# A decoder trunk's mixer: rotary rows exchanged by small transfers instead of a matrix, forget gates placed behind the keys

## The chip, the cores and the metric

One core of a Trainium2 chip. TensorE is called PE, its weight loads PEld, VectorE DVE, ScalarE ACT, GpSimd POOL and SyncE SP; every engine works through its own queue in order. The metric is the time of one execution on the device in microseconds (us), the median of several.

## The reference, cut to what matters

One decoder layer for 256 tokens of width 1024: a norm, a wide input projection, two token mixers side by side (forgetting attention, called fox, with 8 heads, and sparse attention, called nsa, with 8 query heads on 2 key groups), a gated merge, then an expert layer found by product keys, and a last norm. All in float32. The parts that the change touches:

```python
def apply_partial_rope(x, cos, sin):            # of 64 columns of a head the first 16
    xr = x[..., :ROPE_DIM].astype(jnp.float32)
    x1, x2 = xr[..., :half], xr[..., half:]     # 8 and 8
    rot = jnp.concatenate([x1 * c - x2 * s, x1 * s + x2 * c], axis=-1)
    ...
# hybrid_mixer
log_f = jax.nn.log_sigmoid(f_logit + fox_f_bias)         # forget gates, c = cumsum(log_f) in fox_attention
q_nsa = apply_partial_rope(heads(nq, NSA_HEADS), cos, sin)
k_slc = apply_partial_rope(heads(ksl, NSA_GROUPS), cos, sin)
k_win = apply_partial_rope(heads(kwn, NSA_GROUPS), cos, sin)
k_cmp, v_cmp, cmp_end = compress_kv(...)                 # 15 overlapping blocks of 32 tokens through a small MLP
gates = jax.nn.sigmoid(nsa_gate_logit)
```

## The kernel before, in words

Every weight matrix is streamed from memory in blocks of 512 KB. The list `order` (lines 155 to 161) gives their order: the transposed input projections `w_t` (compressed keys and values, selected and window keys, nsa queries, fox queries and keys), natural ones (`w_sv`, `w_fv`), the merge gates `w_m`, and then the branch, output and expert weights up to the end. One call of `slot` (line 228) handles one block: SP fetches blocks two and three ahead into three `raw` buffers, ACT makes the rounded high part `whi` of the block two ahead (L185) and DVE the rest `wlo` (L189), and PE multiplies the present block in three passes (high with high, high with low, low with high), 24 matmuls of 256 columns at L356 for a transposed block. `pair` takes two blocks for one PSUM bank and hands the evacuation of the bank to the list `early`, which runs at the start of the next slot.

All other work of the mixer is put by hand between the blocks: the tuples `pre` that `pair` and `natural` get are functions that run in that slot after the low part and before the slot's matmuls, in the order written. `tick` in a tuple moves the attention heads on by one: it runs first in its slot (before the low part), and issues the values of the head two back, the scores of two new heads on every other call, a softmax on DVE and ACT, and the transposition of the last probabilities. There are 24 heads: 16 nsa heads, which read the rotated queries `nqs`, and 8 fox heads, which add the forget sums `cleft` and `crt` to their scores.

The steps that the change touches, in the order of the slots (lines 783 to 803):

- `start_tables` (L431): the reciprocal norm of each token, spread over the partitions by PE, is copied three times from PSUM by DVE (L347, L433, L434), and the cosine and sine tables are multiplied by it (L435, L436).
- `rope_in` (L452): ACT evacuates a pair (selected and window keys "k", query halves "q0" and "q1"), the tile `ropein`. `rope` (L457): PE multiplies it by a signed exchange matrix `rt` (L460, PSUM out), DVE multiplies that by the sine table (L462) and the evacuated rows by the cosine table (L463), adds them (L465), and `halve` makes the high part on ACT (L449) and the low part on DVE (L450). `swap` (L468) then copies the keys' two halves of the partitions into each other by two transfers on POOL's queue.
- The compression: `cmp_windows` (DVE, L481) lays out the 15 overlapping windows of the keys and of the values, `cmp_hidden` (PE L488, ACT L492) is the first layer with weights that `w1_load` brings by four transfers of 512 KB on SP's queue, `back` (L496) transposes the hidden layer on PE; `cmp_keys`, `cmp_values`, `cmp_scores`, `cmp_turn` and `cmp_out` (L703, two matmuls at L706) follow.
- The forget gates: `fg_log`, `fg_rest` (the reciprocals of the gates and the remainder of the logarithm, L561 to L567), `fg_logs`, `fg_sums` (four matmuls at L578, copies on ACT, low parts on DVE at L584) and eight `fg_left` (L587), one masked copy of the sums for each fox head.

In the kernel before, the pair "q0" has `fg_rest`, the keys' rotary, `swap`, the second windows and the third load in its second slot; the pair "q1" has the two hidden layers, with the transposition of the first (`cmp_back`) ahead of the second, and q0's rotary; the first fox pair has `fg_sums` and q1's rotary.

Of the kernel before, what the change touches and what calls it, by code (L numbers as in the profile page):

```python
# [19 lines left out]
P = 128  # L20
# [17 lines left out]
def _constants():  # L38
# [3 lines left out]
    for b in (0, 64):  # L42
        for i in range(8):
            rt[b + 8 + i, b + i] = -1.0
            rt[b + i, b + 8 + i] = 1.0
    inv = np.power(f(500000.0), -np.arange(0, 16, 2, dtype=f) / f(16)).astype(f)

    def table(pos):
        ang = pos.astype(f)[:, None] * inv[None, :]
        c = np.ones((P, len(pos)), f)  # L50
        s = np.zeros((P, len(pos)), f)
        for b in (0, 64):
            for o in (0, 8):
                c[b + o:b + o + 8] = np.cos(ang).T
                s[b + o:b + o + 8] = np.sin(ang).T
        return c, s
# [75 lines left out]
def body(tc, nc, a):  # L132
# [12 lines left out]
    def bank(tag):  # L145
        return ps.tile([P, 512], F32, name=tag, tag=tag)

    def halves(t):
        return t.rearrange("p (j t) -> p j t", j=2)
# [192 lines left out]

    def spread(r, out):
        rb = bank("pO")
        for b in range(2):
            nc.tensor.transpose(rb[:, b * P:(b + 1) * P], r[:, b:b + 1].to_broadcast([P, P]), ident)
        nc.vector.tensor_copy(out, rb[:, :T])  # L347
        return rb
# [82 lines left out]
    def start_tables():  # L431
        rb = spread(rn[0], rs)
        nc.vector.tensor_copy(rsk[0:64], rb[0:64, :T])  # L433
        nc.vector.tensor_copy(rsk[64:128, 0:T - 1], rb[64:128, 1:T])  # L434
        nc.vector.tensor_tensor(ctab, ctab, rs, OP.mult)  # L435
        nc.vector.tensor_tensor(stab, stab, rs, OP.mult)  # L436
# [11 lines left out]
    def halve(hi, lo, src):  # L448
        nc.scalar.activation(hi, src, AF.Copy)  # L449
        nc.vector.tensor_tensor(lo, src, hi.bitcast(F32), OP.subtract)  # L450

    def rope_in(name, pj, scale):  # L452
        raw = wk.tile([P, 2, T], F32, name="ropein")
        nc.scalar.activation(raw, halves(pj), AF.Copy, scale=scale)
        ropes[name] = raw

    def rope(name, dst, parts):  # L457
        raw = ropes[name]
        rp = bank("pS")
        nc.tensor.matmul(rp, K["rt"], flat(raw), start=True, stop=True)  # L460
        t = wk.tile([P, 2, T], F32, name="ropetmp", bufs=1)
        nc.vector.tensor_tensor(t, halves(rp), stab[:, None, :].to_broadcast([P, 2, T]), OP.mult)  # L462
        nc.vector.tensor_tensor(raw, raw, ctab[:, None, :].to_broadcast([P, 2, T]), OP.mult)  # L463
        dst = raw if dst is None else dst
        nc.vector.tensor_tensor(dst, raw, t, OP.add)  # L465
        halve(*parts, dst)
# [18 lines left out]
    def cmp_hidden(j):  # L485
# [10 lines left out]
        def back():  # L496
            tp = bank("pO")
            nc.tensor.transpose(tp[:, :30], hn, ident[:30, :30])
            nc.vector.tensor_copy(ht[j], tp[:, :30])
        backs.append(back)  # L500

    backs = []

    def cmp_back():
        run(backs)

# [52 lines left out]

    def fg_rest():  # L560
        nc.vector.tensor_scalar(gate, gate, 1.0, None, OP.add)  # L561
        nc.vector.reciprocal(gate, gate)
        nc.vector.tensor_scalar(yr, y1, -1.0, None, OP.add)
        nc.vector.tensor_tensor(ea, ea, yr, OP.subtract)
        nc.vector.reciprocal(yr, y1)
        nc.vector.tensor_tensor(ea, ea, yr, OP.mult)
        nc.vector.tensor_scalar(z, z, 0.0, None, OP.min)  # L567
# [134 lines left out]

    def cmp_out():  # L703
        for b in range(2):
            o = bank("pT")
            nc.tensor.matmul(o, cptb[:, b], flat(vbd), start=True, stop=True)  # L706
            nc.scalar.activation(y[:, b, 1], o, AF.Copy)

# [69 lines left out]
    def sv_evac(acc):  # L778
# [10 lines left out]
    pair(lambda pj: rope_in("q0", pj, 0.125), ah, al,  # L789
         pre=((fg_log, lambda: cmp_windows(0)), (lambda: table(AF.Gelu), fg_rest, lambda: rope("k", None, (krope[:, 0, 0], krope[:, 1, 0])), swap, lambda: cmp_windows(1), lambda: w1_load(1, 0))))  # L790
    pair(lambda pj: rope_in("q1", pj, 0.125), ah, al,
         pre=((lambda: cmp_hidden(0), fg_logs, lambda: w1_load(1, 1)), (cmp_back, lambda: cmp_hidden(1), lambda: rope("q0", nqt[:, 0:2], (nqs[:, 0, 0:2], nqs[:, 1, 0:2])))))
    lefts = [lambda h=h: fg_left(h) for h in range(H)]
    pair(fox_evac(fqt, 0, 0.125), ah, al, ((), ()),
         ((cmp_keys, fg_sums, cmp_back, tick, cmp_copies), (tick, lambda: rope("q1", nqt[:, 2:4], (nqs[:, 0, 2:4], nqs[:, 1, 2:4])))))
    pair(fox_evac(fqt, 1, 0.125), ah, al, ((), ()), ((cmp_keys_rope, tick), (cmp_values, tick, lefts[0])))
    pair(fox_evac(fkt, 0, 1.0), ah, al, ((), ()), ((tick, cmp_scores), (tick, lefts[1], lefts[2])))
    pair(fox_evac(fkt, 1, 1.0), ah, al, ((), ()), ((tick, cmp_turn, lefts[3]), (tick, cmp_out, lefts[4], lefts[5])))
    natural(512, (0, 2, 4, 6, 8), value_evac(vf, 512), lambda k: (),
            lambda k: ((tick, lefts[6]), t2, t2, (tick, lefts[7]))[k])  # L800
    for m in range(8):
        pre = [[tick], [tick]]
        if m == 5:
            pre = [[tick, lambda: y_turn(1, 0)], [tick, lambda: y_turn(1, 1)]]
# [503 lines left out]
```

## Time and profile before

| | us |
|---|---|
| median of 3 runs | 1036.61 |
| lowest, highest | 1035.8, 1037.08 |
| the profiled execution, its own time | 1037.04 |
| span of its profile, first to last instruction | 1035.3 |
| PE busy in the span | 1024.0 |
| DVE, ACT, POOL busy in the span | 768.2, 526.3, 17.9 |

The granted clock of PE is 0.997 of full speed over the span. Busy times of engines lie side by side and do not add up to the span. A matmul's duration contains its passage through the array, so matmuls in a row overlap, and the distance of two starts tells more than a duration. The mixer's part with the pairs listed above lies between about 20 and 175 us; what follows are PE-bound projections and the expert layer.

### The profile page before, as it was taken

Reading aid. Unit: us, or ns where it says so; the run is one execution under the profiler, and the core shown is the slowest. Engines: PE = TensorE matmul, PEld = TensorE weight load, DVE = VectorE, ACT = ScalarE, POOL = GpSimd, SP = SyncE. Lnnn points to the kernel's source line nnn. Section 1 sums busy time; section 2 is a strip of 40 time slices with the busy share of each in tenths; the row PEclk is TensorE's granted clock in tenths of the full one; section 3 lists DMA queues with packets and bytes.
Section 4 is the critical chain, followed back from the end, with each engine's and each line's share of the span. In section 5 each row is a group of like instructions: output and inputs, shape, how many; then the busy total and the mean of one; then the engine's idle time right before and its main releaser. Section 6 shows DMA issues by size and latency. Waiting matters only on the chain.

```text
span 1035.3 us, 18645 instructions
## 1 busy us (share of the span) xinstructions
PE 1024.0 (99%) x7369; PEld 947.8 (92%) x7369; DVE 768.2 (74%) x1454; ACT 526.3 (51%) x841; POOL 17.9 (2%) x31
## 2 busy tenths in 40 slices
PE   9999999999999999999999999999999999999997
PEld 7898999999999999999999999988888888888885
DVE  5788677876798879779889999966666666666664
ACT  7554445565644464644444444445454545555554
POOL 3000010000000000000000000000000000000000
PEclk9999999999999999999999999999999999999998
DMA  8733444566455546554444445445555555555662
GB/s 268 242 101 104 123 121 128 174 189 202 150 189 192 182 152 204 168 199 163 161 149 159 150 159 164 163 163 190 196 192 195 192 195 194 192 197 189 199 208 102
DMA packets 51319, 180.09 MB, mean 174 GB/s; under 512 B 5808, under 2 KB 7232, under 8 KB 51232
## 3 DMA queue, kind: packets, MB, share of 16 engines
q1 hardware_dynamic: 48816, 175.27, 51.8%
q0 software_dynamic: 832, 1.99, 0.8%
q10 hardware_dynamic: 1584, 1.64, 0.5%
q8 instruction: 58, 0.95, 0.4%
q14 instruction: 29, 0.24, 0.1%
HBM read 176.79 MB, written 1.05 MB: 172 GB/s over the span
## 4 chain that ended last, share of the span: by engine, by line
PE 93%; DVE 3%; ACT 2%; DMA 1%; issue 1%; SPq 0%; DVEq 0%; ACTq 0%
PE pj L356 50%; PE acc L1208 34%; PE pw L1161 3%; PE pS L647 1%; PE pT L619 1%; PE pS L488 1%; PE pS L1069 1%; DMA raw<-in_w_t 1%; DVE wlo L189 1%; DMA xg<-in_x 1%; ACT whi L185 1%; PE pO L630 0%; PE pO L631 0%; PE pj L749 0%; PE pj L750 0%
## 5 line engine op out<-in xcount | busy, mean ns | idle before, releaser
L189 DVE TENSOR_TENSOR wlo<-raw,whi 128x1024 fp32r<-128x1024 f32 (+2 forms) x329 | 398.9, 1213 | 133.6 <-ACT whi L185 132.6
L185 ACT ACTIVATE whi<-raw 128x1024 fp32r<-128x1024 f32 (+2 forms) x329 | 342.9, 1044 | 164.7 <-PE pj L356 123.6
L356 PE MATMUL pj<-ah,whi 128*128 128x256 f32 x1344 | 336.1, 288 | 0.0
L356 PE MATMUL pj<-al,whi 128*128 128x256 f32 x1344 | 329.9, 283 | 0.1
L356 PEld LDWEIGHTS pj<-al,whi 128*128 128x128 f32 x1344 | 257.4, 192 | 1.8 <-issue 1.0
L356 PEld LDWEIGHTS pj<-ah,whi 128*128 128x128 f32 x1344 | 257.0, 191 | 1.5 <-issue 1.2
L356 PE MATMUL pj<-ah,wlo 128*128 128x256 f32 x1344 | 189.1, 283 | 0.0
L356 PEld LDWEIGHTS pj<-ah,wlo 128*128 128x128 f32 x1344 | 173.6, 192 | 0.0
L1208 PE MATMUL acc<-whi,ch 128*128 128x512 f32 x512 | 158.5, 389 | 0.0
L1208 PE MATMUL acc<-whi,cl 128*128 128x512 f32 x512 | 158.5, 389 | 0.0
L1208 PE MATMUL acc<-wlo,ch 128*128 128x512 f32 x512 | 158.2, 389 | 0.0
L1196 ACT ACTIVATE ch<-G 128x256 fp32r<-128x256 f32 x128 | 53.4, 418 | 171.2 <-PE acc L1208 171.2
L1208 PEld LDWEIGHTS acc<-whi,cl 128*128 128x128 f32 x512 | 96.1, 188 | 20.3 <-DVE cl L1197 0.3
L1208 PEld LDWEIGHTS acc<-whi,ch 128*128 128x128 f32 x512 | 96.0, 188 | 20.1 <-ACT ch L1196 0.3
L1208 PEld LDWEIGHTS acc<-wlo,ch 128*128 128x128 f32 x512 | 96.1, 188 | 19.9
L1197 DVE TENSOR_TENSOR cl<-G,ch 128x256 fp32r<-128x256 f32 x128 | 54.4, 425 | 69.5 <-ACT ch L1196 69.5
L1173 ACT ACTIVATE G<-pw 128x512 f32<-128x512 f32 (+31 forms) x32 | 12.5, 392 | 73.5 <-DVE G L1171 73.5
L356 PE MATMUL pj<-bh,whi 128*128 128x256 f32 x192 | 48.1, 286 | 0.0
L356 PE MATMUL pj<-bl,whi 128*128 128x256 f32 x192 | 47.5, 283 | 0.0
L1153 DVE TENSOR_TENSOR oha<-oha,wt 128x1024 f16<-128x1024 f16 x64 | 44.3, 692 | 2.2
L356 PEld LDWEIGHTS pj<-bl,whi 128*128 128x128 f32 x192 | 36.8, 192 | 0.0
L356 PEld LDWEIGHTS pj<-bh,whi 128*128 128x128 f32 x192 | 36.8, 192 | 0.0
(278 smaller groups left out, 824.7 us busy)
## 6 DMA issues: line engine op xcount, KB each, us to landing
raw<-in_u_t SPq DMA_DIRECT2D x128, 512.0 KB, 3.4
raw<-in_v_n SPq DMA_DIRECT2D x128, 512.0 KB, 3.2
raw<-in_w_m SPq DMA_DIRECT2D x16, 512.0 KB, 3.6
raw<-in_w_q SPq DMA_DIRECT2D x16, 512.0 KB, 3.8
raw<-in_w_t SPq DMA_DIRECT2D x15, 512.0 KB, 4.6
raw<-in_w_b SPq DMA_DIRECT2D x8, 512.0 KB, 3.6
raw<-in_w_o SPq DMA_DIRECT2D x8, 512.0 KB, 3.5
sg<-in_w SPq DMA_DIRECT2D x4, 512.0 KB, 6.7
```

The source lines that it names most:

```text
L185: return [lambda s=slice(u, min(v, n)): nc.scalar.activation(hi[:, s], raws[k][:, s], AF.Copy) for u, v in cuts]
L189: nc.vector.tensor_tensor(lo[:, cs], raws[k][:, cs], hi[:, cs].bitcast(F32), OP.subtract)
L356: nc.tensor.matmul(out, (wl if v == 2 else wh)[:, c], (l if v == 1 else h)[:, c], start=(i == 0), stop=(i == len(seq) - 1))
L488: nc.tensor.matmul(hp[:30, :P], flat(wins[j][:, lp // 8, lp % 8]), w1[:, j, lp], start=(lp == 0), stop=(lp == 15))
L619: nc.tensor.transpose(pt[:, j * P:(j + 1) * P], self.p[:, j * P:(j + 1) * P], ident)
L647: nc.tensor.matmul(hd.S[:, b * T:b * T + w], qt[:, i, b * P:(b + 1) * P], kt[:, j, :w], start=n == 0 and bias is None, stop=n == 2, skip_g ...
L1153: nc.vector.tensor_tensor(pairs(A[:, s]), pairs(A[:, 1]), same(wt[:, s]), OP.mult)
L1161: nc.tensor.matmul(pw[:, t * P:(t + 1) * P], B[:, t], A[:, s, t], start=(s == 0), stop=(s == 1))
L1173: nc.scalar.activation(G[1][:, n - 64:, ts], pv[:, n:], AF.Copy, scale=1.0 / WSCALE)
L1196: nc.scalar.activation(ch, g, AF.Copy)
L1197: nc.vector.tensor_tensor(cl, g, ch.bitcast(F32), OP.subtract)
L1208: nc.tensor.matmul(acc[2 * b + d], (cl if q == 1 else ch)[:, tb], (vl if q == 2 else vh)[:, cs], start=False, stop=last and q == 2, skip_g ...
```

## The change

The exchange matrix loses its minus sign, and the sine table gets it for the first 8 rows of each 16. `rope` no longer multiplies by the matrix: `rope_in` copies the 8-row groups crosswise by four transfers on POOL's queue, from `ropein` into one buffer `turned`, which is set to zero once and serves all three rotaries; `rope` multiplies `turned` in place by the sine table. (The compressed keys' small rotary, `cmp_keys_rope`, still uses the matrix.) `start_tables` makes its three copies on ACT. The third and fourth loads of the compression weights, the windows, the hidden layers and their transpositions, the parts of the forget gates, the eight masked sums and the two compressed outputs get other places in the slots.

```diff
-            rt[b + 8 + i, b + i] = -1.0
+            rt[b + 8 + i, b + i] = 1.0
...
-                s[b + o:b + o + 8] = np.sin(ang).T
+                s[b + o:b + o + 8] = np.sin(ang).T if o else -np.sin(ang).T
...
-    def spread(r, out):
+    def spread(r, out, copy=nc.vector.tensor_copy):
...
-        nc.vector.tensor_copy(out, rb[:, :T])
+        copy(out, rb[:, :T])
...
     def start_tables():
-        rb = spread(rn[0], rs)
-        nc.vector.tensor_copy(rsk[0:64], rb[0:64, :T])
-        nc.vector.tensor_copy(rsk[64:128, 0:T - 1], rb[64:128, 1:T])
+        copy = lambda o, i: nc.scalar.activation(o, i, AF.Copy)
+        rb = spread(rn[0], rs, copy)
+        copy(rsk[0:64], rb[0:64, :T])
+        copy(rsk[64:128, 0:T - 1], rb[64:128, 1:T])
...
+    turned = p1.tile([P, 2, T], F32, name="turned")
+    nc.gpsimd.memset(turned, 0.0)
+
     def rope_in(name, pj, scale):
         raw = wk.tile([P, 2, T], F32, name="ropein")
         nc.scalar.activation(raw, halves(pj), AF.Copy, scale=scale)
+        for r in (0, 64):
+            for o in (0, 8):
+                nc.gpsimd.dma_start(turned[r + o:r + o + 8], raw[r + 8 - o:r + 16 - o])
         ropes[name] = raw
...
         raw = ropes[name]
-        rp = bank("pS")
-        nc.tensor.matmul(rp, K["rt"], flat(raw), start=True, stop=True)
-        t = wk.tile([P, 2, T], F32, name="ropetmp", bufs=1)
-        nc.vector.tensor_tensor(t, halves(rp), stab[:, None, :].to_broadcast([P, 2, T]), OP.mult)
+        t = turned
+        nc.vector.tensor_tensor(t, t, stab[:, None, :].to_broadcast([P, 2, T]), OP.mult)
...
-    def fg_rest():
+    def fg_gate():
         nc.vector.tensor_scalar(gate, gate, 1.0, None, OP.add)
         nc.vector.reciprocal(gate, gate)
+
+    def fg_rest():
...
-    def cmp_out():
-        for b in range(2):
-            o = bank("pT")
-            nc.tensor.matmul(o, cptb[:, b], flat(vbd), start=True, stop=True)
-            nc.scalar.activation(y[:, b, 1], o, AF.Copy)
+    def cmp_out(b):
+        o = bank("pT")
+        nc.tensor.matmul(o, cptb[:, b], flat(vbd), start=True, stop=True)
+        nc.scalar.activation(y[:, b, 1], o, AF.Copy)
...
     pair(lambda pj: rope_in("q0", pj, 0.125), ah, al,
-         pre=((fg_log, lambda: cmp_windows(0)), (lambda: table(AF.Gelu), fg_rest, lambda: rope("k", None, (krope[:, 0, 0], krope[:, 1, 0])), swap, lambda: cmp_windows(1), lambda: w1_load(1, 0))))
+         pre=((fg_log, lambda: cmp_windows(0), lambda: w1_load(1, 0)),
+              (lambda: table(AF.Gelu), lambda: cmp_windows(1), lambda: rope("k", None, (krope[:, 0, 0], krope[:, 1, 0])),
+               swap, lambda: w1_load(1, 1))))
     pair(lambda pj: rope_in("q1", pj, 0.125), ah, al,
-         pre=((lambda: cmp_hidden(0), fg_logs, lambda: w1_load(1, 1)), (cmp_back, lambda: cmp_hidden(1), lambda: rope("q0", nqt[:, 0:2], (nqs[:, 0, 0:2], nqs[:, 1, 0:2])))))
-    lefts = [lambda h=h: fg_left(h) for h in range(H)]
+         pre=((lambda: cmp_hidden(0),),
+              (lambda: cmp_hidden(1), lambda: cmp_back(0),
+               lambda: rope("q0", nqt[:, 0:2], (nqs[:, 0, 0:2], nqs[:, 1, 0:2])))))
+    left = lambda h: lambda: fg_left(h)
     pair(fox_evac(fqt, 0, 0.125), ah, al, ((), ()),
-         ((cmp_keys, fg_sums, cmp_back, tick, cmp_copies), (tick, lambda: rope("q1", nqt[:, 2:4], (nqs[:, 0, 2:4], nqs[:, 1, 2:4])))))
-    pair(fox_evac(fqt, 1, 0.125), ah, al, ((), ()), ((cmp_keys_rope, tick), (cmp_values, tick, lefts[0])))
-    pair(fox_evac(fkt, 0, 1.0), ah, al, ((), ()), ((tick, cmp_scores), (tick, lefts[1], lefts[2])))
-    pair(fox_evac(fkt, 1, 1.0), ah, al, ((), ()), ((tick, cmp_turn, lefts[3]), (tick, cmp_out, lefts[4], lefts[5])))
+         ((cmp_keys, lambda: cmp_back(1), tick, cmp_copies),
+          (tick, lambda: rope("q1", nqt[:, 2:4], (nqs[:, 0, 2:4], nqs[:, 1, 2:4])))))
+    pair(fox_evac(fqt, 1, 0.125), ah, al, ((), ()), ((cmp_keys_rope, tick, fg_gate), (cmp_values, tick)))
+    pair(fox_evac(fkt, 0, 1.0), ah, al, ((), ()), ((tick, cmp_scores), (tick, fg_rest)))
+    pair(fox_evac(fkt, 1, 1.0), ah, al, ((), ()), ((tick, cmp_turn, fg_logs), (tick, lambda: cmp_out(0))))
     natural(512, (0, 2, 4, 6, 8), value_evac(vf, 512), lambda k: (),
-            lambda k: ((tick, lefts[6]), t2, t2, (tick, lefts[7]))[k])
+            lambda k: ((tick, lambda: cmp_out(1)), (tick, fg_sums), (tick, left(0)), (tick, left(1)))[k])
     for m in range(8):
         pre = [[tick], [tick]]
+        if m < 3:
+            pre = [[tick, left(2 * m + 2)], [tick, left(2 * m + 3)]]
```

(`cmp_hidden` files its transposition under its number, and `cmp_back(j)` calls that one.)

## Rows read from the trace of the kernel before

**Rows 1.** The page, part 1: busy us, share of the span, instructions

```profile
PE 1024.0 (99%) x7369; PEld 947.8 (92%) x7369; DVE 768.2 (74%) x1454; ACT 526.3 (51%) x841; POOL 17.9 (2%) x31
```

**Rows 2.** Windows: busy us of PE, PEld, DVE, ACT, POOL, clock, DMA share, GB/s

```profile
20.00:40.00 20.00, 19.50 (x159) 18.58 (x158) 14.94 (x31) 11.76 (x18) 0.00 (x0) 1.00 0.88 294
40.00:60.00 20.00, 18.91 (x146) 16.65 (x145) 15.19 (x33) 10.51 (x24) 1.17 (x2) 1.00 0.46 129
...
120.00:140.00 20.00, 20.00 (x181) 19.47 (x179) 15.15 (x31) 9.75 (x25) 1.88 (x2) 1.00 0.36 106
```

**Rows 3.** Waits of PE, 15 to 110 us: total us, times, longest

```profile
PE pO L498 <- ACT hn L492: 0.8, 1, 0.8
PE pT L706 <- DVE probt L621: 0.6, 1, 0.6
PE pS L488 <- DVE win L481: 0.5, 1, 0.5
```

**Rows 4.** Timeline of PE around 30 us: start, us, line, operation, tiles, count

```profile
29.58 0.52 PE L356 MATMUL pj<-ah,wlo 128*128 128x256 f32 x3
29.93 1.02 PE L460 MATMUL pS<-ropein,ka 128*128 128x512 f32 x2
30.39 0.68 PE L356 MATMUL pj<-ah,whi 128*128 128x256 f32 x1
30.91 0.28 PE L356 MATMUL pj<-al,whi 128*128 128x256 f32 x1
```

**Rows 5.** Timeline of DVE, 27 to 81 us

```profile
27.68 0.42 DVE L347 COPY rs<-pO 128x256 f32<-128x256 f32 x1
...
28.87 0.43 DVE L435 TENSOR_TENSOR kb<-kb,rs 128x256 f32<-128x256 f32 x1
...
36.12 0.18 DVE L561 TENSOR_SCALAR gate<-gate 128x48 f32<-128x48 f32 x1
...
37.52 0.68 DVE L462 TENSOR_TENSOR ropetmp<-pS,kb 128x512 f32<-128x512 f32 x1
38.12 0.68 DVE L463 TENSOR_TENSOR ropein<-ropein,kb 128x512 f32<-128x512 f32 x1
...
40.22 0.69 DVE L450 TENSOR_TENSOR bl<-ropein,bl 128x512 fp32r<-128x512 f32 x1 [0.70 <-ACT bl L449]
40.83 1.16 DVE L481 TENSOR_TENSOR win<-kcb,pos 128x120 f32<-128x120 f32 x4
41.90 1.22 DVE L189 TENSOR_TENSOR wlo<-raw,whi 128x1024 fp32r<-128x1024 f32 x1
...
46.77 0.69 DVE L462 TENSOR_TENSOR ropetmp<-pS,kb 128x512 f32<-128x512 f32 x1 [1.86 <-PE pS L460]
...
54.17 0.42 DVE L584 TENSOR_TENSOR csb<-pT,csh 8x256 fp32r<-8x256 f32 x1 [0.84 <-ACT crt L582]
...
80.52 0.61 DVE L587 TENSOR_SCALAR cleft<-csb,ka 128x256 fp32r<-128x256 f32 x2
```

**Rows 6.** Timeline of ACT: the evacuations of "k" and "q0"

```profile
28.08 0.58 ACT L454 ACTIVATE ropein<-pj 128x512 f32<-128x512 f32 x1
...
40.10 0.58 ACT L454 ACTIVATE ropein<-pj 128x512 f32<-128x512 f32 x1
```

**Rows 7.** Timeline of POOL: the first exchange of the key halves

```profile
41.21 0.58 POOL L469 DMA_DIRECT2D bl<-bl  x1 [21.38 <-DVE bl L450]
```

**Rows 8.** DMA issues, 0 to 60 us: count, KB each, median us to landing

```profile
kcb<-kraw POOLq DMA_DIRECT2D x2, 127.5 KB, 6.0
...
ident<-in_k_id POOLq DMA_DIRECT2D x1, 64.0 KB, 2.4
fb<-in_f_bias POOLq DMA_DIRECT2D x1, 4.0 KB, 3.0
```

**Rows 9.** Timeline of PE: the matmuls of the forget sums

```profile
51.25 1.11 PE L578 MATMUL pT<-kb,lf 128*128 128x256 f32 x4
```

**Rows 10.** Tile raw on SP, fetches issued 18 to 34 us

```profile
DMA to landing us min/median/max: 4.3/5.6/6.8
```

More of the change, by code (lines that the diff above doesn't have):

```diff
@@ L499, in back, with cmp_back @@
             nc.vector.tensor_copy(ht[j], tp[:, :30])
[L500 to L505, printed above, removed]
+        backs[j] = back
+    backs = {}
+    def cmp_back(j):
+        backs[j]()
     kc = wk.tile([P, 30], F32, name="kc", bufs=1)
```

## Prediction, written before the changed kernel was run

> **What bounds the kernel now.** I began with the shares of the page: PE is busy for 1024.0 us, 99% of the span [rows 1]. So a change can only pay where PE works for nothing or stands still. The windows of 20 us say where that can be: from about 120 us on PE has no gap at all, while from 20 to 60 us it has gaps of 0.5 and 1.1 us in 20, with DVE beside it for 15 us and ACT for 11 to 12 [rows 2]. The change touches only the stretch from 25 to 125 us; behind it the work is the same, PE-bound, and simply starts earlier or later. The gain is therefore the PE work taken out of that stretch, plus PE waits removed there, less PE waits added. PE's list of waits gives those of today: 0.8 us for the hidden layer of the compression (ACT), 0.6 us at the second compressed output and 0.5 us for the first windows (DVE) [rows 3].
>
> **Rotation matmul out.** In PE's timeline two instructions of L460 start at 29.93, the projection after them at 30.39 and its second matmul at 30.91, where projection matmuls normally start 0.12 apart (three of 0.28 each take 0.52 together, since they overlap) [rows 4]. The rotation so costs 30.91 - 29.93 - 0.12 = 0.86 us of PE. There are three (keys, q0, q1): 2.6 us. DVE's three operations per rotary remain; the first now reads SBUF where it read PSUM, and the rows show 0.68 for either source (L462 from PSUM, L463 from SBUF [rows 5]), so I take no change there.
>
> **Rotary by transfers, keys.** Each rotary now waits for four small transfers of 8 rows of 2 KB, issued on POOL's queue right behind the evacuation. For the keys they have time. DVE reached the keys' rotary at 37.52. Ahead of it now go: less the three table copies moved to ACT, 27.68 to 28.87, 1.19; less the forget-gate group, 36.12 to 37.52, 1.40; plus the second windows moved ahead, 40.83 to 41.90, 1.07 [rows 5]. That makes 37.52 - 1.19 - 1.40 + 1.07 = 36.0. The keys' evacuation ended at 28.7 [rows 6] and moves by up to half a microsecond, because ACT now makes the copies first; POOL starts 0.3 us behind what it waited for (41.21, the low part having ended at 40.91) and takes 0.58 an issue [rows 5, 7], so the fourth transfer is issued near 31.2 and has 4.8 us to land. The copies on ACT hide behind DVE's low part of the same weight block; uncovered they would cost about what they save on DVE. The gap at the first windows (0.5) goes with the same 1.19.
>
> **Rotary by transfers, q0.** This is the step that decides. After the keys' rotary starts on DVE, the q0 evacuation on ACT started 40.10 - 37.52 = 2.58 later, and the last low part on DVE (40.22, 0.69) ended 3.39 later [rows 5, 6]. In the change these are 38.6 and 39.4. POOL first issues the two exchanges of the key halves, which wait for that low part: 0.3 us behind it, at 39.7, and 0.58 each [rows 7], to 40.9. The four small ones are queued behind them on the same engine, so the fourth is issued at 40.9 + 3 x 0.58 = 42.6, though the q0 rows were ready at 39.2. The buffer they write was last read by the keys' rotary at 38.0: no wait from that. How long a transfer of 16 KB takes on this queue no row shows alone. The nearest by size are 64 KB in 2.4, 4 KB in 3.0; the longest of the same queue is 6.0 for 128 KB while weights stream [rows 8]. I take 3.0 (a small one issued behind another, as here), with ends 2.4 and 6.0. It lands at 45.6, and DVE starts q0's rotary at 45.65 instead of 46.77: **1.1 us earlier** [rows 5].
>
> Here the Trainium skill has a price, on the page "DMA: Bandwidth & Descriptors", section "Anatomy of one DMA — SWDGE (gpsimd) path": about 2.0 us fixed for a transfer issued from GpSimd, plus bytes over 436 GB/s. By that estimate 16 KB land in 2.04 us and the gain is 1 us larger; no row of this trace is that short.
>
> PE is faster than that. Before its first scores it loses two rotations (1.7), the 0.5 and the 0.8 (the hidden matmuls of the values now stand ahead of the transposition that waited). It would be there about 3 us earlier, but these scores read q0 rotated, and the chain from the start of the rotary (three DVE operations, high part on ACT, low part on DVE) is as long as before. So PE's 3 us come back as a wait of about 2 us, and 1.1 remains. Behind the waiting DVE instruction stand the softmax of the first head and the next low parts; behind the waiting high part on ACT stand the q1 evacuation and a weight block.
>
> **From the first scores to 90 us.** PE loses the third rotation, 0.86, and the 0.6 at the compressed output, because the two outputs now stand in different slots. The four matmuls of the forget sums (1.1) [rows 9] only move behind 93 us, where they cost the same. DVE loses the two low parts of the sums and the wait before them: 0.84 + 2 x 0.42 = 1.7 [rows 5], PE 0.86 + 1.1 = 2.0 in the same slots; at the next copy of transposed probabilities, where the two meet, PE will wait 0.2 to 0.3 more. Into the slots up to 85 us come the gate group, 1.40, and out of them go three of the masked sums, 0.3 each (two hold 0.61) [rows 5]: DVE is 0.5 fuller where it is the later engine, and PE waits that much at the compressed output. Balance: 0.86 + 0.6 - 0.25 - 0.5 = **0.7**. The remaining masked sums move behind 100 us, under PE-bound slots: nothing.
>
> **Compression weights.** Two of the four loads of 512 KB move one slot earlier on SP's queue, each behind a weight fetch and ahead of the next one. SP waits for buffers there, so its 0.4 us of issue are free. The bytes are the same, but come while the queue is full: weight blocks there took between 4.3 and 6.8 us to land [rows 10]. I take nothing, with ends 0 and 2.5 (rival "weights"). The zeroing of the new buffer falls ahead of POOL's first transfers, where an engine with 17.9 us of work in all [rows 1] stands idle: nothing; if it took longer than that gap, it would delay the windows.
>
> **Sum.** 1.1 + 0.7 = 1.8 us. The profiled execution took 1037.04 us against the median of 1036.61; from the former the change gives 1035.2, from the median **1034.8**.
>
> **Rivals.**
> *No price behind the scores.* If the waits of PE for DVE between 60 and 85 us do not grow, or the transfers land in 2.4 or less, 0.6 to 1.7 are added: 2.4 to 3.9 in all, at the middle 3.1, 1033.5. For it: DVE's share there is not full. Against it: the sums above make DVE the later engine in those slots.
> *Transfers too slow (slower).* If the small transfers take the 6.0 of the longest row, the keys' rotary starts at 31.2 + 6.0 = 37.2, 1.2 late; q0's at 42.6 + 1.2 + 6.0 = 49.8, 3.1 later than today; and q1's waits 2 us more, as its evacuation follows q0's high part. Less the 0.7 this is 4.4 slower: 1041.0. It turns to a loss at some 4.5 us a transfer. Against it: the row of 6.0 is of 128 KB each around 20 us, where the DMA engines were busy for 0.88 of the time, against 0.46 from 40 to 60 [rows 2]. The Trainium skill speaks for it: the page "SBUF — State Buffer", section "SBUF: two separate sides", warns that GpSimd cannot write descriptors while DVE holds the shared port in a two-port operation. By that rule the issues would stretch beside DVE; the trace disagrees so far, since the exchange at 41.21 took 0.58 while DVE ran the additions of the windows [rows 5, 7].
> *Weights late.* If the weight block fetched just ahead of the third load lands after 6.8 instead of 4.3 [rows 10], the low part ahead of the keys' rotary, and with it the q0 chain, is late by at most the difference, 2.5: 1.8 - 2.5 = -0.7, at worst 1037.3, at the middle no change.
> *Relief lost.* DVE alone sets the pace behind the first scores, and the 0.7 are lost: gain 1.1, 1035.5. It lies inside the forecast's own span, 0.8 to 2.4.
>
> **Numbers.** The forecast's mechanism (landing 2.4 to 4, gain 0.8 to 2.4) gets 0.55, the second group 0.25, slow transfers 0.12, late weights 0.08. About 0.2% (2.07 us) is what a measurement of this kernel can tell from no change; 1.8 lies just inside. Of the 0.55 some 0.17 is above it: faster 0.17 + 0.25 = 0.42; same 0.38 + 0.08 + 0.02 = 0.48; slower 0.10. The range takes in the best of the second group (3.9) and the end of late weights with a little of slow transfers: 1032.7 to 1037.4.
>
> **What would show it.** PE's waits should list the first scores behind DVE or ACT with about 2 us, and no more the hidden layer or the second compressed output. DVE should wait for a landing ahead of q0's rotary, near 45.6, and not ahead of the keys'. L460 is gone. I am wrong if DVE waits for transfers elsewhere, if the small issues take clearly more than 0.58, or if PE shows no wait at the first scores.

## The result and the profile after

The change made the kernel **slower**: 1042.21 us median of five runs (1040.83 to 1042.84) against 1036.61, a ratio of 1.0052 with a 95% interval of 1.0037 to 1.0067. The forecast was 1034.8, and the range ended at 1037.4. The profiled execution took 1042.21 us itself, with a span of 1040.4 where before had 1035.3, so the 5.1 us are all in the trace.

PE is busy for as long as before, so the loss is standing still or slow work. First the page of the changed kernel, part 1, beside [rows 1]:

```profile
PE 1023.6 (98%) x7363; PEld 949.6 (91%) x7363; DVE 768.4 (74%) x1451; ACT 526.9 (51%) x844; POOL 24.3 (2%) x44
```

PE's waits from 15 to 115 us (total, times, longest), beside [rows 3], and the first of DVE's for the same stretch:

```profile
PE pS L654 <- ACT bh L450: 6.2, 1, 6.2
PE pO L636 <- DVE probt L628: 0.6, 1, 0.6
PE pS L654 <- DVE bh L451: 0.2, 1, 0.2
PE pT L712 <- DVE cptb L708: 0.2, 1, 0.2
```

```profile
DVE turned L467 <- DMA turned<-ropein: 7.7, 2, 4.9
```

The three waits of [rows 3] are gone, as forecast. In their place PE waits 6.2 us once, at L654, the first scores, for the high part of q0; and DVE waits twice, 7.7 us in all, for the small transfers. DVE's timeline shows where, with the rows that answer to L462 in [rows 5]:

```profile
38.19 0.69 DVE L467 TENSOR_TENSOR turned<-turned,kb 128x512 f32<-128x512 f32 x1 [2.80 <-DMA turned<-ropein]
...
49.65 0.69 DVE L467 TENSOR_TENSOR turned<-turned,kb 128x512 f32<-128x512 f32 x1 [4.86 <-DMA turned<-ropein]
...
62.38 0.69 DVE L467 TENSOR_TENSOR turned<-turned,kb 128x512 f32<-128x512 f32 x1
```

The keys' rotary could have started at 38.19 - 2.80 = 35.39 and q0's at 44.79; both stood for data. POOL's timeline (beside [rows 7]) says when the transfers left, and the list of DMA issues (count, KB each, median us to landing), cut to 28 to 32 us, to 41.5 to 45 us and to 52.5 to 55 us, how long they took, for the keys, q0 and q1:

```profile
29.04 2.06 POOL L461 DMA_DIRECT2D turned<-ropein  x4 [9.18 <-issue]
41.89 0.60 POOL L474 DMA_DIRECT2D bl<-bl  x1 [10.79 <-DVE bl L451]
...
43.08 2.02 POOL L461 DMA_DIRECT2D turned<-ropein  x4
```

```profile
raw<-in_w_t SPq DMA_DIRECT2D x2, 512.0 KB, 7.3
sg<-in_w SPq DMA_DIRECT2D x1, 512.0 KB, 8.6
turned<-ropein POOLq DMA_DIRECT2D x4, 16.0 KB, 6.6
...
raw<-in_w_t SPq DMA_DIRECT2D x2, 512.0 KB, 5.1
bl<-bl POOLq DMA_DIRECT2D x2, 256.0 KB, 3.7
turned<-ropein POOLq DMA_DIRECT2D x4, 16.0 KB, 4.9
...
turned<-ropein POOLq DMA_DIRECT2D x4, 16.0 KB, 3.1
```

Medians: 16 KB took 6.6 us while two weight blocks and a load of compression weights were underway, 4.9 behind the exchange and beside two weight blocks, and 3.1 with no weights beside. One by one the trace has the keys' fourth issued at 30.60 and landed at 38.06 (7.5 us), q0's fourth at 44.59 and 49.53 (4.94).

The wait is not all. PE's timeline around the first scores and the projections of the next slot, then the windows of 2 us (busy us of PE, PEld, DVE, ACT, POOL, granted clock, DMA share, GB/s):

```profile
52.39 0.48 PE L654 MATMUL pS<-bl,bh 64*128 64x128 f32 x2 [6.23 <-ACT bh L450]
53.11 1.44 PE L654 MATMUL pS<-bl,bh 64*128 64x128 f32 x10 [0.25 <-DVE bh L451]
...
55.66 0.41 PE L356 MATMUL pj<-al,whi 128*128 128x256 f32 x1
55.87 0.41 PE L356 MATMUL pj<-ah,whi 128*128 128x256 f32 x1
...
60.70 0.28 PE L356 MATMUL pj<-al,whi 128*128 128x256 f32 x1
60.81 0.28 PE L356 MATMUL pj<-ah,whi 128*128 128x256 f32 x1
```

```profile
46.00:48.00 2.00, 0.16 (x2) 0.00 (x0) 0.00 (x0) 0.00 (x0) 0.00 (x0) 1.00 0.93 352
48.00:50.00 2.00, 0.00 (x0) 0.00 (x0) 0.35 (x1) 0.00 (x0) 0.00 (x0) 0.90 0.42 145
50.00:52.00 2.00, 0.00 (x0) 0.00 (x0) 1.64 (x3) 0.29 (x1) 0.00 (x0) 0.50 0.00 0
...
60.00:62.00 2.00, 2.00 (x19) 2.00 (x18) 1.23 (x2) 1.01 (x5) 0.00 (x0) 1.00 0.00 0
```

Read the clock column downwards: PE stood from 46, and from 49.59 to 59.83 (the trace's clock records) the granted clock is 0.50, the lower level of 1.2 GHz. Projection matmuls in that stretch start 0.21 apart (55.66, 55.87), and 0.11 apart behind it (60.70, 60.81). The same two places in the kernel before, by PE's timeline:

```profile
50.23 0.84 PE L647 MATMUL pS<-bl,bh 64*128 64x128 f32 x10 [0.33 <-DVE bh L450]
...
56.74 0.28 PE L356 MATMUL pj<-al,whi 128*128 128x256 f32 x1
```

So the first scores came 53.11 - 50.23 = 2.9 us later, and the second projection matmul of the second slot behind them 60.70 - 56.74 = 4.0 later, although a rotation and four matmuls of the forget sums (0.86 + 1.1) had left that stretch. The slow clock so cost some 1.1 + 2.0 = 3.1 us. Matched matmul by matmul, the lag is 4.4 us behind the wait of 0.6 at L636 and a constant 4.8 from 118 us to the end of the expert layer; what is left of the 5.1 arises at the end of the kernel.

Two more things in these rows. The windows show what the 20-us average of [rows 2] hid: the DMA engines are busy for 0.93 of the time from 46 to 48, just while q0's rows are underway. The kernel before already had such a stretch where the forecast put these transfers (42.6 to 45.6):

```profile
44.00:46.00 2.00, 2.00 (x17) 1.69 (x15) 0.91 (x2) 0.27 (x2) 0.00 (x0) 1.00 0.97 227
```

And the keys' lateness is handed on: the exchange waits for the keys' rotary, and q0's evacuation stands on ACT behind the keys' high part (40.24, then 40.78), so q0's transfers leave only at 43.08 to 44.59.

### The profile page after: what moved, and what is told of

The parts are those of the page before. It is cut to its first block, busy times and chain, and to the rows that moved or that the text cites. A ratio compares the mean times of both kernels' runs of the same rounds, so it can differ in the third digit from the quotient of the medians.

```text
span 1040.4 us, 18654 instructions
## 1 busy us (share of the span) xinstructions
PE 1023.6 (98%) x7363; PEld 949.6 (91%) x7363; DVE 768.4 (74%) x1451; ACT 526.9 (51%) x844; POOL 24.3 (2%) x44
## 4 chain that ended last, share of the span: by engine, by line
PE 92%; DVE 3%; DMA 2%; issue 1%; ACT 1%; POOL 0%; DVEq 0%; ACTq 0%
PE pj L356 50%; PE acc L1221 34%; PE pw L1174 3%; DMA turned<-ropein 1%; PE pS L654 1%; DVE wlo L189 1%; PE pT L626 1%; PE pS L1082 1%; PE pO L637 0%; PE pO L638 0%; DMA raw<-in_w_t 0%; PE pj L755 0%; PE pj L756 0%; PE pj L758 0%; PE pO L636 0%
```

## The experiments

My theory: q0's transfers land late, PE waits at the first scores, and the clock falls behind that wait; everything else in the change helps. Two theories of why they land late: **A**, GpSimd's queue itself is slow or long (the exchange of 512 KB stands ahead in it); **B**, weights are streamed beside them. Each group of kernels was measured beside the kernel before, whose medians were 1036.97 (e1 to e4), 1037.01 (e5 to e8), 1036.96 (e9, e10) and 1036.67 (e11, e12).

**e1, the matrix back, all moves kept.** The rotation is done by the matrix for the names in the tuple; e6, e8 and e11 differ only in it.

```diff
+        if name not in ('k', 'q0', 'q1'):
             for r in (0, 64):
                 for o in (0, 8):
                     nc.gpsimd.dma_start(turned[r + o:r + o + 8], raw[r + 8 - o:r + 16 - o])
...
+        if name in ('k', 'q0', 'q1'):
+            rp = bank("pS")
+            nc.tensor.matmul(rp, K["rt"], flat(raw), start=True, stop=True)
...
+        src = halves(rp) if name in ('k', 'q0', 'q1') else t
+        nc.vector.tensor_tensor(t, src, stab[:, None, :].to_broadcast([P, 2, T]), OP.mult)
```

> The changed kernel with the exchange matrix in place of the small transfers for all three rotaries; every other move of the change (table copies on ACT, slots of loads, gates, sums, outputs) stays. Theory (late transfers): in the changed kernel q0's rotary started on DVE at 49.65 instead of 46.77, because its fourth transfer landed 4.9 us after its issue, and PE stood still for 6.2 us before the first scores and then worked at half clock. Without transfers that wait is gone: q0's rotary at about 44.6, first scores about 2 us earlier than in the kernel before, total 1034 to 1036, so a little faster than before. Rival (the slots): the moved work is what costs; then it stays above 1039.

1034.67 (ratio 0.998, 0.997 to 0.9989). DVE's row of q0's rotary:

```profile
44.79 0.69 DVE L472 TENSOR_TENSOR turned<-pS,kb 128x512 f32<-128x512 f32 x1 [0.87 <-PE pS L469]
```

PE's waits from 15 to 115 us are down to 0.3 + 0.2. The moves alone gain 2.3 us, with the clock full; q0's rotary starts 2.0 earlier than in [rows 5]. The transfers turn that gain into a loss: 7.5 us between this kernel and the changed one.

**e2, the transfers alone**, put into the kernel before with nothing moved.

```diff
+                nc.gpsimd.dma_start(turned[r + o:r + o + 8], raw[r + 8 - o:r + 16 - o])
...
-        nc.tensor.matmul(rp, K["rt"], flat(raw), start=True, stop=True)
```

> The kernel before with the small transfers alone; all slots as before. Theory (late transfers): slower than before by about as much as the whole change, 1041 to 1045, with a wait of PE for the first scores of 4 us or more and a drop of the granted clock behind it. Rival (the slots): 1035 to 1037.

1040.57 (1.0042, 1.0028 to 1.0056). The direction is the expected one; the time is just under what I gave, and PE's wait well under it, though the profiled execution, at 1039.8, was the quickest of the five:

```profile
PE pS L651 <- ACT bh L449: 2.2, 1, 2.2
```

```profile
48.12 0.69 DVE L466 TENSOR_TENSOR turned<-turned,kb 128x512 f32<-128x512 f32 x1 [3.29 <-DMA turned<-ropein]
```

The keys' rotary (37.45) waits for nothing here, since their transfers landed in 3.1 to 3.9 us, with the loads of compression weights in their former slots; q0's still waits 3.29. The clock is low for 3.41 us.

**e3, PE kept busy**: 28 matmuls that nothing reads, ahead of the first scores.

```diff
+    def fill():
+        fb2 = bank("pO")
+        for _ in range(28):
+            nc.tensor.matmul(fb2, warm[:, :P], warm, start=True, stop=True)
...
-    pair(fox_evac(fqt, 0, 0.125), ah, al, ((), ()),
+    pair(fox_evac(fqt, 0, 0.125), ah, al, ((fill,), ()),
```

> The changed kernel with 28 matmuls of zeros (128 by 512, results not used) put into PE's wait before the first scores; they should take about 6 us there and end about when the scores can start. Theory (the low clock is a part of the loss of its own): the granted clock stays at 1.0, the projection matmuls behind the scores start 0.12 apart instead of 0.21, and about 3 us come back: 1038.5 to 1040. Rival (the late rotary alone, through DVE's and ACT's chain): the clock stays high, but the total stays at 1041.5 to 1042.5.

1039.24 (1.0021, 1.0012 to 1.003). q0's rotary waits as long as ever (next row), but the clock stays full through the scores: the fall costs 1042.2 - 1039.2 = 3.0 us, as worked out above (3.1).

```profile
50.28 0.69 DVE L467 TENSOR_TENSOR turned<-turned,kb 128x512 f32<-128x512 f32 x1 [5.18 <-DMA turned<-ropein]
```

**e4, the third and fourth loads of compression weights in their former slots.**

```diff
-          pre=((fg_log, lambda: cmp_windows(0), lambda: w1_load(1, 0)),
+          pre=((fg_log, lambda: cmp_windows(0)),
...
-               swap, lambda: w1_load(1, 1))))
+               swap, lambda: w1_load(1, 0))))
...
-         pre=((lambda: cmp_hidden(0),),
+         pre=((lambda: cmp_hidden(0), lambda: w1_load(1, 1)),
```

> The changed kernel with the third and fourth load of the compression weights in their former slots. Theory (sharing of the DMA engines with any weight stream): the keys' transfers land sooner (about 5 us instead of 7.5 for the last), the keys' rotary starts 1 to 2 us earlier, q0's by as much, total 1039 to 1042. Rival (the moved loads are the whole reason why transfers are late): the keys' transfers cost no wait and the total falls to 1036 to 1037.

1040.97 (1.0043, 1.0029 to 1.0056), not clearly apart from the changed kernel. In the trace the step is plain: the keys' rotary waits 1.07 instead of 2.80 and everything behind it is 1.4 earlier, but q0's wait is as long as before. But five other kernels with the keys' transfers and these loads as in the changed one (e3, e7 to e10) have the fourth landing after 5.8 to 6.0 us and a wait of 1.5 to 1.7, so 2.80 was the reading of one slower execution, and the loads' own share is some 0.5 us. They explain nothing of q0's wait.

```profile
36.66 0.69 DVE L467 TENSOR_TENSOR turned<-turned,kb 128x512 f32<-128x512 f32 x1 [1.07 <-DMA turned<-ropein]
...
48.28 0.69 DVE L467 TENSOR_TENSOR turned<-turned,kb 128x512 f32<-128x512 f32 x1 [4.88 <-DMA turned<-ropein]
```

**e5, all small transfers issued by SP.**

```diff
-                nc.gpsimd.dma_start(turned[r + o:r + o + 8], raw[r + 8 - o:r + 16 - o])
+                nc.sync.dma_start(turned[r + o:r + o + 8], raw[r + 8 - o:r + 16 - o])
```

> The changed kernel with all small transfers issued by SP instead of POOL, so neither POOL's 0.5 us an issue nor the exchange stands ahead of q0's. Theory A (queue order on POOL): q0's land near 45, 4 us earlier than in the changed kernel, 1036 to 1038. Theory B (weight traffic at the same time): those of the keys, among weights, stay late by 5 us or more, those of q0 land about 1.5 us earlier than before, 1039 to 1041. Rival C (transfers of 8 rows are slow by themselves on any queue): landing 4.5 us or more everywhere, q1's too.

1035.23 (0.9986, 0.9977 to 0.9995; single runs from 1033.81 to 1038.07). Better than either theory gave. SP's timeline and DVE's rows:

```profile
28.71 2.80 SPq L461 DMA_DIRECT2D turned<-ropein  x4
...
38.84 3.01 SPq L461 DMA_DIRECT2D turned<-ropein  x4
41.89 1.33 SPq L174 DMA_DIRECT2D raw<-in_w_t  x2
```

```profile
35.65 0.69 DVE L467 TENSOR_TENSOR turned<-turned,kb 128x512 f32<-128x512 f32 x1
...
44.27 0.69 DVE L467 TENSOR_TENSOR turned<-turned,kb 128x512 f32<-128x512 f32 x1 [0.91 <-DMA turned<-ropein]
```

On SP's queue the small transfers are not beside the weights but ahead of them: the loads and fetches are issued behind, on the same queue. The keys wait for nothing, so q0's leave 4.2 us earlier than in the changed kernel, beside the exchange and not behind it, and ahead of the two fetches. That removes both suspected causes at once, and GpSimd's way of issuing with them, so it doesn't tell A from B.

**e6, transfers for q1 alone**, and **e8, the matrix for q0 alone**; against e1, in all three places:

```diff
-        if name not in ('k', 'q0', 'q1'):
+        if name not in ('k', 'q0'):
...
-        if name not in ('k', 'q0', 'q1'):
+        if name not in ('q0',):
```

> The changed kernel with the matrix for the keys and q0 and the small transfers for q1 alone. In every run so far q1's transfers cost DVE no wait, and alone on the engines they landed 2.2 to 3.1 us after their issue. Theory (late transfers, and q0's are the ones that cost): the third rotation's 0.86 us of PE goes on top of what the version with the matrix for all three (1034.7) gained: 1033.5 to 1034.3, and no new wait of PE. Rival (any such transfer costs on its way, by POOL's issues or the buffer): 1035 or more.

> The changed kernel with the matrix for q0 alone; keys and q1 by small transfers. Theory (q0's wait is the one that costs): the keys' rotary is still 2 to 3 us late on DVE, but q0's can then start near 45, since its matrix waits for no landing; the clock stays high; PE's first scores wait about 1 us longer than with the matrix for all three, which eats the keys' 0.86: 1033.5 to 1035. Rival (the keys' late transfers carry the loss on to q0): 1037 or more.

e6: 1034.84 (0.9976, 0.9967 to 0.9985), above what I gave and no better than e1. q1's transfers landed in a median of 2.2 us, and DVE waited for none of them.

The trace shows where the matmul saved goes. From the last pass of one block to that of the next, PE takes 4.06 us in e1 (51.55 to 55.61) and 3.19 in e6 (52.03 to 55.22): the rotation's 0.87 is gained. Over the next two blocks e1 takes 9.47 (to 65.08) and e6 10.33 (to 65.55): it is all lost again, at a wait for DVE's copy of the probabilities that e1 doesn't have.

```profile
62.03 0.43 PE L641 MATMUL pO<-vsw,probt 128*128 128x64 f32 x2 [0.63 <-DVE probt L633]
```

DVE sets the pace there, so PE's saving is worth nothing.

e8: 1034.3 (0.997, 0.9958 to 0.9981), as expected. The keys' rotary still waits, at 37.62, yet q0's starts as early as in e1:

```profile
37.62 0.69 DVE L472 TENSOR_TENSOR turned<-turned,kb 128x512 f32<-128x512 f32 x1 [1.66 <-DMA turned<-ropein]
...
44.64 0.69 DVE L472 TENSOR_TENSOR turned<-pS,kb 128x512 f32<-128x512 f32 x1 [0.42 <-PE pS L469]
```

A late landing of the keys alone costs nothing that shows. It is q0's transfers that cost.

**e7, the exchange issued behind q0's small transfers.**

```diff
-               swap, lambda: w1_load(1, 1))))
+               lambda: w1_load(1, 1))))
...
-         pre=((lambda: cmp_hidden(0),),
+         pre=((swap, lambda: cmp_hidden(0)),
```

> The changed kernel with the exchange of the key halves (two transfers of 256 KB) issued behind q0's four small ones instead of ahead of them. Theory A (the small ones are late because the exchange stands ahead of them in the same queue): the fourth lands 2.5 to 3.5 us after its issue, near 46.5, PE's wait halves, 1036.5 to 1038.5. Theory B (the weight blocks fetched at the same time make them late): the landing stays at 4.5 to 5 us, only the 1.2 us of the two issues come back, 1039.5 to 1041.

1041.11 (1.0035, 1.0023 to 1.0047). By its time alone this looks as if B were right and A wrong. The trace says otherwise. DMA issues from 41.5 to 43.6 us, then from 43.6 to 45 us:

```profile
turned<-ropein POOLq DMA_DIRECT2D x4, 16.0 KB, 1.7
...
raw<-in_w_t SPq DMA_DIRECT2D x2, 512.0 KB, 6.4
bl<-bl POOLq DMA_DIRECT2D x2, 256.0 KB, 7.0
```

```profile
PE pS L654 <- DMA bl<-bl: 4.2, 1, 4.2
```

With nothing ahead of them in their queue, and issued before the fetches (from 43.70 on), the four landed 1.74 to 1.76 us after issue on GpSimd's own queue, and q0's rotary ran at 45.07. But now the exchange, which the same scores read, was issued behind the first fetch (43.75 and 44.36), took 6.11 and 7.91 us, and PE waited for it instead. The wait only changed its owner.

**e9, the weight fetches held back**: SP reads two rows of the exchanged keys, and so stands until the exchange has landed.

```diff
+    held = p1.tile([2, 64], F32, name="held")
...
+        if name == "q0":
+            nc.sync.dma_start(held, krope[63:65, 0, 1, 0, 0:64].bitcast(F32))
```

> The changed kernel, with one tiny transfer on SP's queue behind q0's evacuation that reads a row pair of the exchanged keys: SP stands until the exchange has landed, so the two weight fetches that ran beside q0's transfers are issued behind it. Nothing on GpSimd's queue moves. Theory B (weights beside them): the exchange lands 3.0 to 3.8 us after its issue, as where no weights ran, q0's fourth transfer 2 to 3 us after its issue instead of 4.94, at 45.5 to 47, and TensorE's wait ahead of the first scores falls from 6.2 us to 2 to 3.5; time 1036.5 to 1039. Theory A (GpSimd's own queue, with the exchange's 512 KB ahead in it): q0's fourth still takes over 4 us, the wait stays over 5 us, and the held fetches cost beside; 1041.5 to 1044.

1039.04 (1.0019, 1.001 to 1.0028), at the upper edge of what B gave. DMA issues from 42 to 45 us, DVE's row and PE's wait:

```profile
bl<-bl POOLq DMA_DIRECT2D x2, 256.0 KB, 3.6
turned<-ropein POOLq DMA_DIRECT2D x4, 16.0 KB, 3.3
```

```profile
47.69 0.69 DVE L470 TENSOR_TENSOR turned<-turned,kb 128x512 f32<-128x512 f32 x1 [2.74 <-DMA turned<-ropein]
```

```profile
PE pS L657 <- ACT bh L450: 2.9, 1, 2.9
```

Without the weights q0's fourth took 2.83 us instead of 4.94, and PE's wait fell from 6.2 to 2.9. The rest is A: the exchange landed at 46.78, 4.13 after its issue, and the four small ones right behind it, at 46.97, 47.17, 47.37 and 47.57. So the exchange and the weights **both** hold a share. From one kernel to the next, the fourth takes 1.74 alone (e7), 2.83 with the exchange ahead (e9), 4.94 with the weights beside as well.

The landings of all kernels fit one order. Wherever the keys' or q0's fourth left GpSimd's queue with large transfers still underway, it landed between 0.2 us ahead of and 1.2 us behind the last of those issued before it, whichever engine had issued that. So it was in 13 of 14 cases; in the other, e2's keys, it landed 2.3 behind. This is read off the landings, not varied in a run of its own.

**e10, q0's four transfers alone on SP's queue.**

```diff
-                nc.gpsimd.dma_start(turned[r + o:r + o + 8], raw[r + 8 - o:r + 16 - o])
+                (nc.sync if name == "q0" else nc.gpsimd).dma_start(turned[r + o:r + o + 8], raw[r + 8 - o:r + 16 - o])
```

> The changed kernel with q0's four transfers alone issued by SP; those of the keys and of q1 stay on GpSimd's queue. On SP's queue q0's transfers stand ahead of the two weight fetches and not behind the exchange. Theory B: the fourth lands 2 to 3 us after its issue, the rotary of q0 waits under 1.5 us, TensorE's wait ahead of the first scores is under 1.5 us and the clock stays full; 1033.5 to 1035.5, as with q0 by the matrix. Theory A with the keys as the cause: the keys' transfers still land late on GpSimd's queue, the exchange and q0's evacuation with them, and the weight fetches are pushed back 2 to 3 us: 1036 to 1039.

1038.3 (1.0016, 1.0007 to 1.0025): the second expectation came true. q0's fourth was issued at 43.92 and its rotary ran 2.9 later, as I had hoped for, but the keys were late again, and with them q0:

```profile
38.25 0.69 DVE L467 TENSOR_TENSOR turned<-turned,kb 128x512 f32<-128x512 f32 x1 [1.59 <-DMA turned<-ropein]
...
46.83 0.69 DVE L467 TENSOR_TENSOR turned<-turned,kb 128x512 f32<-128x512 f32 x1 [1.98 <-DMA turned<-ropein]
```

PE waited 2.3 + 0.4 us.

On SP's queue, too, q0's rotary starts just behind the landing of the exchange (46.45), so nothing here shows that GpSimd's queue by itself is slow. Against e5 both rotaries are 2.6 later (38.25 and 35.65, 46.83 and 44.27), and only the queue of the keys' and q1's transfers differs. The keys' lateness does cost, where q0 goes by transfers.

**e11, transfers for q0 alone**, against e1 in all three places:

```diff
-        if name not in ('k', 'q0', 'q1'):
+        if name not in ('k', 'q1'):
```

> The changed kernel with the matrix back for the keys and q1, and the small transfers for q0 alone, on GpSimd's queue. The keys' rotary then waits for no transfer, so exchange and evacuation of q0 come some 2.5 us earlier than in the changed kernel. If q0's transfers alone cost the time, the fourth still lands over 4 us after its issue (the exchange ahead of it, the two weight fetches from 41.6 us on beside it), TensorE waits 1.5 to 4 us ahead of the first scores and the clock falls: 1036.5 to 1040. If the keys' late landing was the root, and q0's only suffers from it: fourth landing within 3.5 us, wait under 1.2 us, clock full, 1034 to 1035.5.

1039.01 (1.0022, 1.0013 to 1.0031; single runs from 1036.79 to 1040.61), as the first expectation had it: 4.3 us over e1 from q0 alone, 3.2 under the changed kernel. The profiled execution took 1037.18 itself, near the lower end, and even there q0's fourth took 4.38 us:

```profile
46.30 0.69 DVE L472 TENSOR_TENSOR turned<-turned,kb 128x512 f32<-128x512 f32 x1 [1.64 <-DMA turned<-ropein]
```

PE waited 1.5 + 0.4 us ahead of the first scores.

**e12, the matrix for q0, the other small transfers issued by SP**: against e8,

```diff
-                    nc.gpsimd.dma_start(turned[r + o:r + o + 8], raw[r + 8 - o:r + 16 - o])
+                    nc.sync.dma_start(turned[r + o:r + o + 8], raw[r + 8 - o:r + 16 - o])
```

> Small transfers for the keys and q1 issued by SP, the matrix for q0. Put together from the two quickest kernels so far: the keys' transfers go ahead of the compression weights on SP's queue, so the keys' rotary waits under 0.5 us (1.66 with GpSimd's queue), and q0 waits for no transfer. TensorE's waits ahead of the first scores under 0.5 us, clock full; 1033.2 to 1034.8, a little under q0 by the matrix with GpSimd's queue (1034.3). Against it: SP stands at each evacuation and its weight fetches slide back by 2 to 3 us each time, which would show as TensorE waiting for weight halves, and 1035 to 1037.

1034.15 (0.9976, 0.9967 to 0.9985). The keys' rotary ran at 35.14 without a wait, PE waited 0.7 + 0.3 us ahead of the first scores, more than I gave, and the clock was low for 3.41 us in this execution, which took 1035.76, over its kernel's median. It can't be told from e8; SP's queue brings nothing once q0 waits for no transfer.

## Why the prediction was wrong

The step that failed is the landing of the small transfers: 3.0 us for q0's fourth and at most 4.8 for the keys' were written, 4.94 and 7.5 were measured. The cost of the low clock behind the long wait, 3.0 us, stood in no term at all.

**What bounds the kernel, and where the change can act**: right. PE has no waits but those listed, the lag of the changed kernel is constant from 118 us to the end of the expert layer, and e1 shows that moves in this stretch alone are worth 2.3 us.

**Rotation matmul out**: the size was right, 0.87 in e6, but not its worth: q1's is lost again at the next wait for DVE, and of the keys' some 0.4 goes to PE's wait for the first windows (0.4 in e8). The medians don't show it.

**Keys**: DVE was ready at 35.39 (forecast 36.0), the fourth transfer issued at 30.60 (31.2). The 4.8 us left for landing were thought ample; it took 7.5. This is the first step that failed, and the row that would have warned was in hand: 6.0 us for the longest of the queue [rows 8], from the very stretch in which DMA is busy for 0.88 [rows 2]. I used it as an end of q0's range and not for the keys. Moving the loads of compression weights, which I priced by what they do to other weights ("I take nothing"), made it a little worse: 5.45 in e4 against 5.8 to 6.0 in most kernels with the loads moved, and 7.5 in this execution.

**q0**, the step that was said to decide, and did: fourth issue forecast at 42.6, measured 44.59, because the exchange and the evacuation inherited the keys' delay; landing taken as **3.0**, measured **4.94**. Together that is 49.53 where 45.6 was written. I chose 3.0 by the rows nearest in size, and passed over one of just this size in the same list, 0.9 longer:

```profile
pos<-in_pos POOLq DMA_DIRECT2D x1, 16.0 KB, 3.9
```

The runs show that size was the wrong measure: 16 KB took from 1.74 to 7.5 us, by what stood ahead in the queue and what streamed beside it. The argument against the slow rival, a DMA share of 0.46 over 20 us, failed because 20 us is too long a stretch: it is 0.93 in the 2 us that counted, and was 0.97 from 44 to 46 in the kernel before.

**PE at the first scores**: forecast to be there 3 us early and to wait 2. It was there at 46.2 and waited 6.2 + 0.2. The mechanism was right, the size followed from the landing.

**The clock** stood in no step. A wait of this length cost 3.0 us more (e3), which the rival "transfers too slow" lacked too: by its place and mechanism it is what happened, at 1042.2 where it said 1041.0, and it got a chance of 0.12. That its number came so near is luck in part: the 2 us that it gave to q1's wait did not come (62.38, no wait), and the clock's 3.0 stood in their place.

**From the first scores to 90 us**: the compressed output's wait shrinks, from 0.6 to 0.2. The third rotation goes, but PE waits 0.6 for the probabilities where the forecast had 0.2 to 0.3 more, and its 0.86 is lost there (e6), as the rival "relief lost" had it for the whole 0.7.

**Issue times**: 2.02 to 2.06 us for four, so some 0.5 each against 0.58 assumed. The Trainium skill's warning on the shared port ("SBUF — State Buffer", section "SBUF: two separate sides") can't explain q0's lateness: DVE stood idle from 44.79 to 49.65, and the fourth, issued at 44.59, still took 4.94, while e7's took 1.74 beside DVE's low parts. The issues were no longer either. The Trainium skill's price for a GpSimd transfer ("DMA: Bandwidth & Descriptors", section "Anatomy of one DMA — SWDGE (gpsimd) path"), 2.04 us by estimate, is near the 1.74 of e7 and holds for a transfer alone. The rule that applied is another of that page, section "Issuing engines are not separate DMA queues": transfers end up on the same 16 DMA engines and interleave, whichever engine issues them. The runs agree that the engines are shared: 1.74 alone, 4.94 with the exchange ahead and weights beside, and in e10 2.9 from SP's queue with the exchange beside.

**What beats both kernels**: the moves with q0 by the matrix, e8, 0.997 of before, or e12, e6, e1 and, with every transfer on SP's queue, e5, whose intervals overlap with it.

## What to carry to other kernels

A small transfer on the critical path is not priced by its bytes but by the large transfers issued shortly before it, on whichever queue, and by the DMA share of the very microseconds in which it flies, so cut the windows to its length before choosing a row. Where a step waits for a transfer, look at what waits on that step in turn: here the keys' delay reached q0 through the exchange on POOL and the high part on ACT. And a wait of PE that is long enough for the granted clock to fall costs its length plus the slow work behind it; three matmuls were a cheap price for not waiting. PE work saved just ahead of a wait for another engine came back as waiting (e6).

## What the runs showed of the hardware

- Four transfers of 16 KB in a row on GpSimd's queue landed 1.74 to 1.76 us after issue with nothing large issued before them (e7; 1.73 to 1.75 for q1's in e3; 2.7 to 3.6 for q1's in the changed kernel, where in that stretch the list of queues shows one packet of 16 KB on q8, the instructions' queue, and in e3 none), 3.9 to 5.0 behind an exchange and beside two blocks of 512 KB (e11), 5.5 to 7.6 beside three or more of 512 KB (the changed kernel's keys). Behind a large transfer of the same queue they landed within 0.2 us of it and of each other (e9).
- For a large transfer the order of issue counted as well: the exchange's two of 256 KB took 3.09 and 4.13 us with no weight fetches (e9), 3.04 and 4.28 with two issued behind them (the changed kernel), 6.11 and 7.91 issued behind one (e7).
- The granted clock fell to 0.50 for 3.41 us (PE's waits of 1.5 + 0.4 and 2.2 + 0.4 us, e11 and e2), 6.83 (2.3 + 0.4, 2.9 + 0.4, 4.8 + 0.3; e10, e9, e4) and 10.24 (6.2 + 0.2, the changed kernel; 4.2 + 0.5, e7). With waits of 0.8 + 0.4 us (e5) it stayed full, and with 0.7 + 0.3 (e12) it fell for 3.41: the length of the wait alone doesn't tell. These are single executions.
- An issue on SP's queue took 0.62 to 1.21 us for such a small transfer (e5), on GpSimd's 0.50 to 0.55 (the changed kernel); the engine with the longer issues still made the quicker kernel.
